# The seven-product form for w_down in a squared-ReLU MLP, and a reordered form for w_up

## The chip, the cores and the metric

The kernel runs on one core of a Trainium2 chip. The metric is the device time of one launch in microseconds: the median of three runs is 1365.35 us for the kernel before (1364.28 to 1368.06). The tensor engine is written TensorE or PE, its weight loads PEld; VectorE is DVE, ScalarE is ACT, GpSimd is POOL; SP is the engine that issues most transfers (DMAs).

## The reference

The program is one step of a two-layer encoder trunk over 640 tokens with a model width of 1024. Each layer has a mixer, a memory attention, projections, and the MLP that the change is about, with a hidden width of 4096:

```
def squared_relu_mlp(x, g_pre, g_post, w_up, w_down):
    a = jnp.square(jax.nn.relu(rmsnorm(x, g_pre) @ w_up))
    return rmsnorm(a @ w_down, g_post)
```

All data are float32, and the kernel keeps that precision: it splits each operand into a high part in the type fp32r, on which TensorE multiplies, and a low part (the operand less its high part), and forms three matmul terms, low by high, high by high and high by low.

## The kernel before

**Tiling.** Tokens are five tiles of 128 (NT), or two halves of 320 (TH). The hidden width is 32 tiles of 128, taken two at a time as 16 pairs (NPAIR). `mlp` runs once for each layer.

**w_up.** The first two pairs of a layer are multiplied in the plain form (`plain`). The other 14 go through the class `Pair`, which uses the Strassen-Winograd form: with two hidden tiles, two halves of the model width and two halves of the tokens, there would be eight products of blocks; the form takes seven, of sums and differences of blocks. A product (`Pair.product`, L597) is 12 matmuls of 320 columns: three terms by four tiles of depth. `Pair.load` makes the sums of the weights s1 to s4 on VectorE (L585 to L588); `head`, `middle`, `second` and `end` run the seven products into six PSUM banks, copy two of the results out on ScalarE (L604, L609) and add the others up in a tile c on VectorE (L612). `end` then makes the squared relu on VectorE and splits it into high and low part.

**w_down.** `down` is plain: for each of the five token tiles, two halves of the model width, the two hidden tiles of a pair and three terms there is a matmul of 512 columns, 60 for a pair (`token_major`, L181, L183, L185); VectorE adds each of the ten sums into y (L701).

**Splits of weights.** `split` (L512, L513) is a cast on ScalarE and a subtraction on VectorE. `summed_parts` does it without VectorE: ScalarE writes the negated cast into the low part, a DMA issued by GpSimd that adds in flight brings the weights on top, and ScalarE casts again:

```
        nc.scalar.mul(lo[:, :w], raw, -1.0)
        nc.gpsimd.dma_start(out=lo[:, :w], in_=src, accum_op=ALU.add)
        nc.scalar.copy(out=hi[:, :w], in_=raw)
```

**Buffers.** Raw weights of 128 x 1024 land in the ring `wraw` of four buffers, by loads on SP's queue. The sums of `Pair.load` take buffers of the same ring. Split weights go into the ring `wring` of eight. PSUM is six short banks (`bank`, named b) and two long ones (`long_bank`, named o).

**What sets the order.** The loop runs `pair.whole()`, the w_down of the pair before, and the load of the next pair. A scheduler turns the program into one fixed queue for each engine when it is built, with `tc.high_priority` and `tc.issue_after` (in `behind`) as hints; each engine then works its queue strictly in order, and an instruction at its head that waits holds all behind it.

Of the kernel before, what the change touches and what calls it, by code (L numbers as in the profile page):

```python
# [9 lines left out]
F32 = mybir.dt.float32  # L10
# [5 lines left out]
P = 128  # L16
# [21 lines left out]
def trunk_kernel(ctx: ExitStack, tc: tile.TileContext, a: dict, o: dict):  # L38
# [17 lines left out]
    def nm(s):  # L56
        uid[0] += 1
        return f"{s}_{uid[0]}"

    def bank():  # L60
        return ps.tile([P, 512], F32, tag="b", name=nm("b"))

    def long_bank():
        return ps.tile([P, 512], F32, tag="o", bufs=2, name=nm("o"))
# [6 lines left out]
    gfm = const.tile([P, G_END], F32, name="gfm")  # L71
    bfb = const.tile([P, 8], F32, name="bfb")
    mhalf = const.tile([P, 1], F32, name="mhalf")
    memqs = const.tile([P, 4, P], F32, name="memqs")
    nc.vector.memset(mhalf, -0.5)
    warm = const.tile([P, 1], F32, name="warm")
    nc.scalar.activation(out=warm, in_=mhalf, func=AF.Square)
# [134 lines left out]
            marks["dve"] = nc.vector.scalar_tensor_tensor(out=xn, in0=x, scalar=r, in1=gb, op0=ALU.mult, op1=ALU.mult)  # L212
        return xn

    def to_fm(xn, hi, lo, c0):

        for q in range(2):
            acc = bank()
            for k in range(4):
                nc.tensor.transpose(acc[:, k * P:(k + 1) * P], xn[:, (4 * q + k) * P:(4 * q + k + 1) * P], ident)  # L220
            av = acc.rearrange("p (k t) -> p k t", k=4)
            h = hi[:, 4 * q:4 * q + 4, c0:c0 + P]
            nc.scalar.copy(out=h, in_=av)
            nc.vector.tensor_tensor(out=lo[:, 4 * q:4 * q + 4, c0:c0 + P], in0=av, in1=h.bitcast(F32), op=ALU.subtract)  # L224
# [10 lines left out]
        t = 0 if i * P < half[1][0] else 1  # L235
        return t, i * P - half[t][0]

    def tile_to(hs, i, xn, half=HALF, prio=HP):
        t, c0 = where(i, half)
        with tc.high_priority(offset=prio):  # L240
            to_fm(xn, hs[t][0], hs[t][1], c0)

    def gain_tile(cpool, src, tag):
        g = cpool.tile([P, D], F32, tag=tag, bufs=1, name=nm(tag))
# [209 lines left out]
    class OutProj:  # L454
# [32 lines left out]
        def flush(self, parts=None):  # L487

            i, xn = self.late.pop(0)
            with tc.high_priority(offset=HP):  # L490
                views = []
                for q in range(2):
                    acc = bank()
                    for k in range(4):
                        nc.tensor.transpose(acc[:, k * P:(k + 1) * P], xn[:, (4 * q + k) * P:(4 * q + k + 1) * P], ident)  # L495
                    views.append(acc.rearrange("p (k t) -> p k t", k=4))
                if parts:
                    for q in range(2):
                        split(*parts[q], views[q])
                for q in range(2):  # L500
                    dst = self.raw[:, 4 * q:4 * q + 4, i * P:(i + 1) * P]
                    if q == 0:
                        nc.scalar.copy(out=dst, in_=views[q])
                    else:
                        nc.vector.tensor_copy(out=dst, in_=views[q])
# [9 lines left out]
    def mlp(l, proj, x_in, aside, yside, hst, before, finish):  # L515
# [8 lines left out]
        apool = ast.enter_context(pool(f"act{l}", 1, aside))  # L524
        tpool = tst.enter_context(pool(f"blk{l}", 1, aside))

        b1 = (hpool.tile([P, KT, TH], F32R, tag="hi0", name=nm("b1h")), hpool.tile([P, KT, TH], F32R, tag="lo0", name=nm("b1l")))
        b22 = (hpool.tile([P, 4, TH], F32R, tag="hi1", name=nm("b22h")), hpool.tile([P, 4, TH], F32R, tag="lo1", name=nm("b22l")))

        def blk(x, what):  # L530
            return tuple(tpool.tile([P, 4, TH], F32R, tag=f"t{x}{y}", name=nm(f"{what}{y}")) for y in "hl")
# [34 lines left out]
        class Pair:  # L566
# [30 lines left out]
                        nc.tensor.matmul(acc[:, :TH], w[wi][:, k, :], b[bi][:, k, :], start=(f and k == 0), stop=(e and k == 3),  # L597
                                         skip_group_check=not first)

            def head(self):  # L600
                self.t = apool.tile([P, 2, 2, TH], F32, tag="c", bufs=2, name=nm("c"))
                acc = long_bank()
                self.product(self.a11, b11, acc)
                nc.scalar.copy(out=self.t[:, 0, 1, :], in_=acc[:, :TH])  # L604
                self.x = acc

            def second(self):
                self.product(self.a12, b21, self.x, False, True)
                nc.scalar.copy(out=self.t[:, 0, 0, :], in_=self.x[:, :TH])  # L609

            def add(self, out, in0, acc):
                nc.vector.tensor_tensor(out=out, in0=in0, in1=acc[:, :TH], op=ALU.add)  # L612

            def middle(self):
                c12, c21, c22 = self.t[:, 0, 1, :], self.t[:, 1, 0, :], self.t[:, 1, 1, :]
                y, w, self.z = bank(), bank(), long_bank()
                self.product(self.s2, ts[1], y)
                self.add(c12, c12, y)
                self.product(self.s3, ts[2], w)
                self.add(c21, c12, w)  # L620
                self.product(self.s1, ts[0], self.z)
                self.add(c22, c21, self.z)

            def end(self):
                c12, c21 = self.t[:, 0, 1, :], self.t[:, 1, 0, :]
                v = bank()
                self.product(self.a22, ts[3], v)
                self.add(c21, c21, v)
                self.product(self.s4, b22, self.z, False, True)
                self.add(c12, c12, self.z)  # L630
                out = [None, None]
                for x in (1, 0):
                    t = self.t[:, x].rearrange("p h n -> p (h n)")
                    nc.vector.scalar_tensor_tensor(out=t, in0=t, scalar=0.0, in1=t, op0=ALU.max, op1=ALU.mult)
                    out[x] = (apool.tile([P, 640], F32R, tag="ah", bufs=4, name=nm("ah")),
                              apool.tile([P, 640], F32R, tag="al", bufs=4, name=nm("al")))
                    split(*out[x], t)
                return out

            def whole(self):  # L640
                self.head()
                self.middle()
                self.second()
                return self.end()

        ys = []
        gpost = []
# [63 lines left out]
        def plain(pcs, tiles, tmp, h):  # L711

            blocks = (b12, b22) if h else (b11, b21)
            for x, (hi, lo) in enumerate(pcs):
                acc = bank()
                for w, y, first, last in ((hi, 0, True, False), (lo, 0, False, False), (hi, 1, False, True)):
                    for k in range(KT):
                        nc.tensor.matmul(acc[:, :TH], w[:, k * P:(k + 1) * P], blocks[k // 4][y][:, k % 4, :],  # L718
                                         start=(first and k == 0), stop=(last and k == KT - 1))
                r = tmp[x // 2][:, x % 2, h, :]  # L720
                ah, al = (t[:, h * TH:h * TH + TH] for t in tiles[x])
                nc.scalar.activation(out=r, in_=acc[:, :TH], func=AF.Relu)
                nc.scalar.activation(out=ah, in_=r, func=AF.Square)
                nc.vector.tensor_tensor(out=r, in0=r, in1=r, op=ALU.mult)
                nc.vector.tensor_tensor(out=al, in0=r, in1=ah.bitcast(F32), op=ALU.subtract)
                if x == 2 and h == 0:
                    n = 4 * P - TH
                    proj.flush([tuple(y[:, :, n:TH] for y in b) for b in (b12, b22)])


        pcs = [piece(a["w_up"][l, f]) for f in range(4)]
        tiles = [(apool.tile([P, 640], F32R, tag="ah", bufs=4, name=nm("ah")),
                  apool.tile([P, 640], F32R, tag="al", bufs=4, name=nm("al"))) for _ in range(4)]
        tmp = [apool.tile([P, 2, 2, TH], F32, tag="c", bufs=2, name=nm("c")) for _ in range(2)]
        first = dict(marks)
        half_blocks(0, TH)
# [3 lines left out]
        other_blocks()  # L740
        hst.close()
        ypool = yst.enter_context(pool(f"y{l}", 1, yside))
        ready = [tiles[:2], tiles[2:]]
        down((0, 1), ready.pop(0), True, False)
        with behind(*first.values()):
            pair = Pair(2)
            pair.load()
        for c in range(2, NPAIR):
            ready.append(pair.whole())
            if c < NPAIR - 1:  # L750
                down((2 * c - 2, 2 * c - 1), ready.pop(0), False, False)
                pair = Pair(c + 1)
                pair.load()
        tst.close()
        cpool = ast.enter_context(pool(f"chain{3 + l}", 2, aside))
        gpost.append(gain_tile(cpool, a["g_mlp_post"][l], "gp"))
        down(range(2 * NPAIR - 4, 2 * NPAIR), ready[0] + ready[1], False, True)
        yst.close()
        return ast

# [24 lines left out]
    att0 = ExitStack()  # L785
    keep0 = att0.enter_context(pool("keep0", 1))
    memq = keep0.tile([P, 4, 512], F32, name="memq0")
    mk0 = keep0.tile([P, 4, 256], F32, name="mk0")
    mv0 = keep0.tile([P, 2, 512], F32, name="mv0")
    wk = att0.enter_context(pool("wk0", 2))  # L790
# [68 lines left out]
    def windows(g):  # L859
# [10 lines left out]
            nc.gpsimd.tensor_tensor(out=nxt[:, c0:], in0=cur[:, c0:], in1=cur[:, c0 - d:784 - d], op=ALU.add)  # L870
            cur, d = nxt, 2 * d
        sp_, ss_ = u_views(cur)
        head = sm(16, "s16")
        nc.vector.tensor_tensor(out=head, in0=sp_[:, 0:16], in1=cst[:, C_IV + 16 * g:C_IV + 16 * g + 16], op=ALU.mult)
        nc.vector.tensor_tensor(out=head, in0=head, in1=up_[:, 0:16], op=ALU.subtract)
        nc.vector.scalar_tensor_tensor(out=up_, in0=sp_, scalar=1.0 / w, in1=up_, op0=ALU.mult, op1=ALU.subtract)
# [63 lines left out]

    def before0(i):
        if len(late) > 1:
            tile_to(hs1, *late.pop(0), HALF1, 0)

    st1.close()
    st1 = mlp(0, proj, proj.x_out, "left", "right", hst, before0, finish0)
# [26 lines left out]
    fox = ExitStack()  # L973
    fk = fox.enter_context(pool("fk", 1))
    memq = fk.tile([P, 4, 512], F32, name="memq1")
    v = fk.tile([P, 4, 512], F32, name="v1")
    kt = [fk.tile([P, 512], F32, name=f"kt{j}") for j in range(4)]
    q = [fk.tile([P, 512], F32, name="q0")]
# [461 lines left out]
```

## Time and profile before

| | |
|---|---|
| median of three runs | 1365.35 us |
| the profiled execution | 1365.08 us |
| its span | 1363.3 us |
| TensorE busy | 1332.5 us, 98% |
| VectorE busy | 848.0 us, 62% |
| ScalarE busy | 608.8 us, 45% |
| GpSimd busy | 246.5 us, 18% |

The profile is one execution of the program. Busy time counts the operations of an engine and not its waits; the span is the time from the first instruction to the last. The MLP of the second layer runs its pairs in the stretch of 972 to 1230 us, that of the first layer in the same way before it.

### The profile page before, as it was taken

The page shows a single profiled execution, that of the slowest core. Times are in us where ns is not written, and L with a number is a line of the kernel's source. Part 1 is how long each engine was busy: PE and PEld are TensorE (multiplying, and loading weights), DVE is VectorE, ACT ScalarE, POOL GpSimd, SP SyncE. Part 2 cuts the span into 40 slices and gives each one's busy share as a digit, 9 for nine tenths or more (in the row PEclk, how much of TensorE's full clock was granted, in tenths as well). Part 3 has the DMA queues.
Part 4 walks back from the last instruction along what each step waited for, and adds up shares of the span by engine and source line. Part 5 has one row for each costly group of instructions (what it writes and reads, how often), then busy time and mean ns, then how long its engine had stood idle before and what let it go on. Part 6 is the DMA issues. An engine that isn't in the chain of part 4 may idle for free. (4 is left out here: it accounts for less than half of the span.)

```text
span 1363.3 us, 20887 instructions
## 1 busy us (share of the span) xinstructions
PE 1332.5 (98%) x8154; PEld 1175.7 (86%) x8154; DVE 848.0 (62%) x1437; ACT 608.8 (45%) x1015; POOL 246.5 (18%) x252
## 2 busy tenths in 40 slices
PE   7999999999999999998999999999999999999997
PEld 6998878988988998996998786679989988988996
DVE  6657439767557666658634566549766566556646
ACT  6435337544353453444434444447534444443432
POOL 3270002111111111133300212312111111111111
PEclk9999999999999999999999998999999999999999
DMA  7736556575666666575636532736666675675663
GB/s 268 224 84 230 204 199 170 123 170 127 161 160 141 161 143 159 135 201 193 240 128 206 178 117 97 243 126 170 150 152 141 153 167 128 154 167 135 155 155 124
DMA packets 87315, 222.82 MB, mean 163 GB/s; under 512 B 18464, under 2 KB 26144, under 8 KB 87216
## 3 DMA queue, kind: packets, MB, share of 16 engines
q1 hardware_dynamic: 69936, 165.91, 37.0%
q0 software_dynamic: 17280, 55.58, 22.3%
q8 instruction: 64, 1.05, 0.3%
q14 instruction: 35, 0.29, 0.1%
HBM read 203.84 MB, written 17.61 MB: 162 GB/s over the span
## 5 line engine op out<-in xcount | busy, mean ns | idle before, releaser
L155 ACT ACTIVATE wl<-raw 128x1024 fp32r<-128x1024 f32 x120 | 114.9, 959 | 252.5 <-PE b L181 243.5
L181 PE MATMUL b<-wl,ah 128*128 128x512 f32 x632 | 200.1, 397 | 4.8 <-DVE hlo L224 2.0
L701 DVE TENSOR_TENSOR y<-y,b 128x512 f32<-128x512 f32 x278 | 177.9, 680 | 38.6 <-PE b L185 38.2
L183 PE MATMUL b<-wh,ah 128*128 128x512 f32 x632 | 198.0, 394 | 0.0
L185 PE MATMUL b<-wh,al 128*128 128x512 f32 x632 | 198.0, 395 | 0.0
L156 POOL DMA_DIRECT2D wl<-in_w_up x56 | 49.2, 879 | 542.3 <-ACT wl L155 286.8
L181 PEld LDWEIGHTS b<-wl,ah 128*128 128x128 f32 x632 | 117.7, 189 | 32.0 <-ACT ah L512 2.7
L183 PEld LDWEIGHTS b<-wh,ah 128*128 128x128 f32 x632 | 118.9, 188 | 27.7
L185 PEld LDWEIGHTS b<-wh,al 128*128 128x128 f32 x632 | 119.1, 188 | 27.5
L512 ACT CAST wh<-raw 128x1024 fp32r<-128x1024 f32 x56 | 58.8, 1049 | 137.0 <-PE o L597 126.1
L157 ACT CAST wh<-raw 128x1024 fp32r<-128x1024 f32 x120 | 112.8, 940 | 0.0
L612 DVE TENSOR_TENSOR c<-c,b 128x320 f32<-128x320 f32 x84 | 41.0, 488 | 106.3 <-PE b L597 106.3
L148 DVE TENSOR_TENSOR wl<-raw,wh 128x1024 fp32r<-128x1024 f32 (+1 forms) x60 | 77.3, 1299 | 20.0 <-ACT wh L147 19.0
L147 ACT CAST wh<-raw 128x1024 fp32r<-128x1024 f32 (+1 forms) x60 | 62.9, 1049 | 40.8 <-POOL raw L144 11.2
L513 DVE TENSOR_TENSOR wl<-raw,wh 128x1024 fp32r<-128x1024 f32 x56 | 68.6, 1224 | 16.1 <-ACT wh L512 15.4
L144 POOL TENSOR_TENSOR raw<-raw,gfm 128x1024 f32<-128x1024 f32 (+1 forms) x28 | 56.5, 2025 | 101.3 <-issue 47.9
L156 POOL DMA_DIRECT2D wl<-in_w_down x64 | 56.4, 887 | 88.7 <-ACT wl L155 49.0
L200 POOL TENSOR_TENSOR s<-s,mhalf 128x1 f32<-128x1 f32 x40 | 26.2, 654 | 230.9 <-DVE s L448 160.0
L585 DVE TENSOR_TENSOR raw<-raw 128x512 f32<-128x512 f32 x28 | 19.4, 692 | 69.1 <-DMA raw<-in_w_up 69.1
L612 DVE TENSOR_TENSOR c<-c,o 128x320 f32<-128x320 f32 x56 | 27.3, 488 | 46.9 <-PE o L597 46.9
L174 PE MATMUL b<-hhi,wh 128*128 128x384 f32 (+1 forms) x312 | 54.7, 316 | 0.3 <-ACT wh L147 0.3
L181 PE MATMUL b<-wl,cathi 128*128 128x512 f32 x160 | 54.7, 422 | 0.0
(324 smaller groups left out, 2760.7 us busy)
## 6 DMA issues: line engine op xcount, KB each, us to landing
raw<-in_w_up SPq DMA_DIRECT2D x64, 512.0 KB, 4.1
raw<-in_w_down SPq DMA_DIRECT2D x64, 512.0 KB, 5.3
wl<-in_w_down POOLq DMA_DIRECT2D x64, 512.0 KB, 8.3
wl<-in_w_up POOLq DMA_DIRECT2D x28, 512.0 KB, 7.0
raw<-in_w_in SPq DMA_DIRECT2D x16, 512.0 KB, 6.8
raw<-in_w_out SPq DMA_DIRECT2D x16, 512.0 KB, 4.6
t<-in_cmk SPq DMA_DIRECT2D x32, 256.0 KB, 5.6
t<-in_cmv SPq DMA_DIRECT2D x32, 256.0 KB, 4.8
```

Source lines behind the costliest of these rows:

```text
L147: nc.scalar.copy(out=hi[:, :w], in_=raw[:, :w])
L148: nc.vector.tensor_tensor(out=lo[:, :w], in0=raw[:, :w], in1=hi[:, :w].bitcast(F32), op=ALU.subtract)
L155: nc.scalar.mul(lo[:, :w], raw, -1.0)
L156: nc.gpsimd.dma_start(out=lo[:, :w], in_=src, accum_op=ALU.add)
L157: nc.scalar.copy(out=hi[:, :w], in_=raw)
L181: nc.tensor.matmul(accs[q][:, :nh], xh, lo[:, c[q]], start=first, stop=False)
L183: nc.tensor.matmul(accs[q][:, :nh], xh, hi[:, c[q]], start=False, stop=False)
L185: mm = nc.tensor.matmul(accs[q][:, :nh], xl, hi[:, c[q]], start=False, stop=last)
L512: nc.scalar.copy(out=hi, in_=src)
L513: nc.vector.tensor_tensor(out=lo, in0=src, in1=hi.bitcast(F32), op=ALU.subtract)
L612: nc.vector.tensor_tensor(out=out, in0=in0, in1=acc[:, :TH], op=ALU.add)
L701: nc.vector.tensor_tensor(out=yq, in0=yq, in1=accs[q], op=ALU.add)
```

## The change

**w_down in seven products.** For hidden tiles 4 to 27 of each layer, two pairs are now taken together, a turn of the new loop. The four hidden tiles are two blocks by two, the model width two halves of 512, and the first four token tiles two blocks of 256. `Down` makes the sums of the w_down blocks: eight subtractions of 512 columns on VectorE in a turn, into four more buffers of `wraw`, and their splits. `Acts` makes the sums of the activations, on 256 columns. `down_form` runs the seven products for both pairs, 12 matmuls of 512 columns each, and for the fifth token tile 24 plain ones: 108 in a turn, where 120 stood. Each product ends in two adds into y, one for each token tile of a block, and the fifth tile takes two more: 16 adds of 512 columns in a turn where 20 stood.

**w_up's form.** `Pair.products` takes the place of `head` to `end`. The seven products go into three banks; a bank is read (copied by ScalarE, L612, L616, L621) in the middle, and the next product sums on into it. So ScalarE makes three copies of 320 columns and VectorE three adds (L603) instead of two and five, and the squared relu is two operations on ScalarE for each of four blocks (L639, L640, L631, L632).

**Smaller edits.** The first four hidden tiles of w_down run as one block, at the end of which the turns begin; `memqs` and a small tile move to other pools; late transposes go into the long banks, and one is tied behind a named matmul; the tiles of `hpool` are made larger, to hold some of the new operands.

```diff
+            def products(self, acts=None):
+                self.c = apool.tile([P, 2, 2, TH], F32, tag="c", bufs=2, name=nm("c"))
...
+                y, x, z = bank(), bank(), long_bank()
+                self.product(self.a11, b11, y)
+                nc.scalar.copy(out=c11, in_=y[:, :TH])
+                self.product(self.a12, b21, x)
+                self.add(c11, x)
+                self.product(self.s2, ts[1], y, False)
+                nc.scalar.copy(out=c12, in_=y[:, :TH])
+                self.act(c11)
+                if acts:
+                    acts.begin(flat)
+                self.product(self.s1, ts[0], z)
+                nc.scalar.copy(out=c22, in_=z[:, :TH])
+                self.product(self.s3, ts[2], y, False)
+                self.add(c22, y)
+                self.act(c22)
+                self.product(self.s4, b22, z, False)
+                self.add(c12, z)
+                self.act(c12)
...
+                self.product(self.a22, ts[3], y, False)
...
+        class Down:
+            def __init__(self, c):
...
+                for x in range(2):
+                    r = wraw.tile([P, RW], F32, tag="raw", name=nm("raw"))
+                    nc.sync.dma_start(out=r[:, :D], in_=a["w_down"][l, 2 * c + x])
...
+            def sums(self, x):
+                r = wraw.tile([P, RW], F32, tag="raw", name=nm("raw"))
+                p, q = r[:, 0:512], r[:, 512:D]
...
+                if x == 0:
+                    sub(p, self.r12, self.r11)
+                    sub(q, self.r22, p)
...
+            product("a12", "b21", x)
+            adds(0, 0, x)
+            product("s1", "t1", z)
+            adds(2, 1, z)
+            product("s2", "t2p", y, False)
+            adds(0, 1, y)
...
+        for c in range(2, NPAIR, 2):
+            end = c == NPAIR - 2
+            dws = []
+            acts = [plain_acts(two[0].products(), 0) if end else two[0].products(Acts(0))]
+            if not end:
+                dws = [Down(c)]
+                t12, t34 = dws[0].sums(0), dws[0].sums(1)
+                dws[0].plain()
+                dws.append(Down(c + 1))
+                dws[1].plain()
+                dws[0].t1, dws[0].t2p = parts(t12[:, :D])
+            acts.append(plain_acts(two[1].products(), 1) if end else two[1].products(Acts(1)))
+            if not end:
+                t12 = dws[1].sums(0)
...
+                down_form(acts, dws)
```

**The order on the engines.** ScalarE before, from the splits of the summed weights of one pair to those of the next two tiles of w_down. The names are tile<-source with a buffer number; L155 is the negated cast, L157 the second cast, and c<-o copies a bank.

```order
L512 CAST wh_12212<-raw_12206 128x1024 [waits DVE_49,PE_49]
L604 COPY c_11996<-o_11997 128x320 [waits PE_49]
L512 CAST wh_12216<-raw_12207 128x1024 [waits DVE_49,PE_49]
L155 ACTIVATE wl_12221<-raw_12204 128x512 [waits DMAHW1_49,DMASW6_49,PE_49]
L609 COPY c_11996<-o_11997 128x320 [waits PE_49]
L157 CAST wh_12220<-raw_12204 128x512
L155 ACTIVATE wl_12335<-raw_12332 128x1024 [waits DMAHW2_49,DMASW7_49,PE_49]
L157 CAST wh_12334<-raw_12332 128x1024 [waits PE_49,Activation_49]
L155 ACTIVATE wl_12342<-raw_12339 128x1024 [waits DMAHW3_49,DMASW5_49,PE_49]
```

Only two copies from banks stand among these, near their head. In the kernel after, ScalarE in the second half of a turn's first pair, where the third w_down tile (raw_11550) and the fourth (raw_11552) are split, up to the first copy from a bank of the turn's second pair (the c_11571 of L612):

```order
L154 ACTIVATE wl_11555<-raw_11550 128x1024 [waits DMAHW4_49,DMASW2_49,PE_49]
L639 ACTIVATE c_11412<-c_11412 128x320 [waits DVE_49]
L156 CAST wh_11554<-raw_11550 128x1024 [waits PE_49]
...
L632 ACTIVATE c_11412<-c_11412 128x320 [waits Activation_49]
L154 ACTIVATE wl_11560<-raw_11552 128x1024 [waits DMAHW5_49,DMASW1_49]
L511 CAST ah_11409<-c_11412 128x512 [waits Activation_49]
L511 CAST ah_11409<-c_11412 128x256 [waits DVE_49]
L511 CAST ah_11409<-st_11411 128x512 [waits DVE_49]
L156 CAST wh_11559<-raw_11552 128x1024
L511 CAST wh_11564<-raw_11534 128x1024 [waits PE_49]
L612 COPY c_11571<-b_11572 128x320
```

Two negated casts, each of which waits for the load of its tile (DMAHW), now stand ahead of the copy by which TensorE may go on in that bank.

VectorE before, at the loads of a pair (L585 to L588) among the adds into y of the w_down that runs meanwhile:

```order
L585 TENSOR_TENSOR raw_12206<-raw_12204 128x512 [waits DMAHW6_49,DMAHW1_49]
L701 TENSOR_TENSOR y_1_9593<-y_1_9593,b_11888 128x512 [waits PE_49]
L513 TENSOR_TENSOR al_11871<-c_11767,ah_11870 128x640 [waits Activation_49]
L701 TENSOR_TENSOR y_1_9593<-y_1_9593,b_11889 128x512 [waits PE_49]
L586 TENSOR_TENSOR raw_12206<-raw_12206,raw_12197 128x512 [waits DMAHW0_49,DVE_49]
L701 TENSOR_TENSOR y_1_9610<-y_1_9610,b_11904 128x512 [waits PE_49]
```

The same place after, for the second pair of a turn to come (raw_11388 is its second w_up tile), among the adds into y (L722) of the last products of w_down:

```order
L722 TENSOR_TENSOR y_1_9779<-y_1_9779,b_11222 128x512 [waits PE_49]
L722 TENSOR_TENSOR y_1_9750<-y_1_9750,b_11225 128x512 [waits DVE_49,PE_49]
L512 TENSOR_TENSOR wl_11373<-raw_11363,wh_11372 128x1024 [waits Activation_49]
L722 TENSOR_TENSOR y_1_9779<-y_1_9779,b_11226 128x512 [waits DVE_49,PE_49]
L722 TENSOR_TENSOR y_1_9808<-y_1_9808,b_11221 128x512 [waits PE_49]
L587 TENSOR_TENSOR raw_11390<-raw_11388 128x512 [waits DMAHW1_49,Activation_49]
L589 TENSOR_TENSOR raw_11391<-raw_11381,raw_11388 128x512 [waits DMAHW0_49,DVE_49]
L722 TENSOR_TENSOR y_1_9837<-y_1_9837,b_11222 128x512 [waits PE_49]
```

The sums of the weights have moved from among the first adds of a pair's w_down to a place ahead of the last adds of a turn, and the first pair's low part (wl_11373) stands before them.

## Rows read from the trace of the kernel before

**Rows 1.** The page: busy time of each engine, its share of the span, instructions.
```profile
PE 1332.5 (98%) x8154; PEld 1175.7 (86%) x8154; DVE 848.0 (62%) x1437; ACT 608.8 (45%) x1015; POOL 246.5 (18%) x252
```
**Rows 2.** Busy us by stretch: length, PE, PEld, DVE, ACT, POOL, granted clock, DMA share, GB/s.
```profile
972.00:1100.00 128.00, 128.00 (x707) 115.25 (x706) 80.32 (x122) 54.80 (x69) 17.63 (x20) 1.00 0.65 154
```
**Rows 3.** Waits, 972 to 1230: engine, line, releaser: us in total, times, longest.
```profile
ACT wl L155 <- PE b L181: 79.2, 9, 9.0
...
DVE raw L585 <- DMA raw<-in_w_up: 26.7, 10, 3.7
...
PEld b L181 <- DVE y L701: 0.8, 2, 0.4
```
**Rows 4.** The chain of waits: by line, then in order of time (start, us).
```profile
by line: PE o L597 7.0%; PE b L181 6.2%; PE b L183 6.0%; PE b L185 6.0%; PE b L597 5.3%; PE b L718 1.5%; DMA raw<-in_w_up 0.7%; DMA xr<-x 0.6%; issue 0.4%; DVE xr L451 0.4%; PE b L495 0.3%; POOL s L200 0.3%; PE o L1288 0.3%; PE b L1269 0.3%
...
1025.65 1.75 PE o L597 x12
...
1209.12 1.75 PE o L597 x12
```
**Rows 5.** Groups of instructions by form: busy us, mean ns of one | idle before.
```profile
L701 DVE TENSOR_TENSOR y<-y,b 128x512 f32<-128x512 f32 x278 | 177.9, 680 | 38.6 <-PE b L185 38.2
...
L513 DVE TENSOR_TENSOR wl<-raw,wh 128x1024 fp32r<-128x1024 f32 x56 | 68.6, 1224 | 16.1 <-ACT wh L512 15.4
L512 ACT CAST wh<-raw 128x1024 fp32r<-128x1024 f32 x56 | 58.8, 1049 | 137.0 <-PE o L597 126.1 <-PE b L185 8.3 <-DVE raw L586 2.6
...
L513 DVE TENSOR_TENSOR al<-c,ah 128x640 fp32r<-128x640 f32 x56 | 45.7, 818 | 0.8 <-ACT ah L512 0.8
...
L612 DVE TENSOR_TENSOR c<-c,b 128x320 f32<-128x320 f32 x84 | 41.0, 488 | 106.3 <-PE b L597 106.3
...
L325 DVE TENSOR_SCALAR mp<-mp,s 128x256 f32<-128x256 f32 x32 | 9.9, 350 | 0.9
...
L723 ACT ACTIVATE ah<-c 128x320 fp32r<-128x320 f32 x16 | 7.5, 470 | 0.3
```
**Rows 6.** Timeline at 1007 to 1009: start, us, engine, line, operation [idle before].
```profile
1007.37 1.23 DVE L513 TENSOR_TENSOR wl<-raw,wh 128x1024 fp32r<-128x1024 f32 x1 [0.60 <-ACT wh L512]
...
1008.62 0.80 SPq L576 DMA_DIRECT2D raw<-in_w_up  x2
```
**Rows 7.** Raw loads by line, 972 to 1230; last row: two loads at 1191.
```profile
L162 SPq DMA_DIRECT2D raw<-in_w_down x20: 327/328/328, 972.8 to 1211.5; - x20
DMA to landing us min/median/max: 4.7/5.3/6.8
...
L576 SPq DMA_DIRECT2D raw<-in_w_up x20: 327/350/827, 982.5 to 1218.9; - x20
DMA to landing us min/median/max: 3.6/3.7/7.7
...
DMA to landing us min/median/max: 3.8/5.7/7.7
```
**Rows 8.** Timeline of 1009 to 1037: VectorE, ScalarE and TensorE at a pair's start.
```profile
1022.32 0.68 DVE L588 TENSOR_TENSOR raw<-raw,raw 128x512 f32<-128x512 f32 x1
1022.92 3.82 DVE L701 TENSOR_TENSOR y<-y,b 128x512 f32<-128x512 f32 x6
...
1023.38 1.06 ACT L155 ACTIVATE wl<-raw 128x1024 fp32r<-128x1024 f32 x1 [9.02 <-PE b L181]
1024.35 1.03 ACT L157 CAST wh<-raw 128x1024 fp32r<-128x1024 f32 x1
...
1027.25 0.74 PE L597 MATMUL b<-t1h,wh 128*128 128x320 f32 x4
...
1027.45 0.43 ACT L604 COPY c<-o 128x320 f32<-128x320 f32 x1 [0.71 <-PE o L597]
```
**Rows 9.** The page: DMAs that add in flight, issued by GpSimd: KB each, us to landing.
```profile
wl<-in_w_down POOLq DMA_DIRECT2D x64, 512.0 KB, 8.3
wl<-in_w_up POOLq DMA_DIRECT2D x28, 512.0 KB, 7.0
```

## What the change does to the time, predicted before the run

> **What bounds the kernel now.** I read the busy shares first: TensorE is busy 98% of the span, VectorE 62%, ScalarE 45% [rows 1]. Then the stretch in which the MLP of the second layer runs its pairs: in 972 to 1100 us TensorE is busy for all 128.00 us at full granted clock, VectorE for 80.32 and ScalarE for 54.80 [rows 2]. In the waits of 972 to 1230 TensorE has one row, 0.8 us; ScalarE's multiplications of w_down tiles (L155) wait for TensorE alone, for buffers it still reads, and none of them has a row for a transfer; only VectorE waits for one, 26.7 us ahead of L585 [rows 3], and as TensorE goes on meanwhile, that costs nothing. So the pair is bound by TensorE's work. The chain in order of time gives its length: the product of L597 that opens a pair comes back every (1209.12 - 1025.65)/7 = 26.21 us [rows 4]. Seven products of twelve matmuls at 1.76 us [rows 4] are 12.3 us, so the 60 matmuls of 512 columns of w_down take 13.9, or 0.231 us each.
>
> **The change, part by part.** I take two pairs, one turn of the new loop, as the unit: 52.4 us before. There are six turns in a layer, twelve in all.
>
> Removed on TensorE: 108 matmuls of 512 columns stand where 120 stood. A turn of matmuls alone is 14 x 1.76 + 108 x 0.231 = 49.6 us, 2.8 less, and 12 x 2.8 = 33 us in all. That is what the change offers.
>
> Added on VectorE, per turn: 8 sums of w_down blocks and 4 low parts of 512 columns (0.68 each), 4 low parts of 1024 (1.22) and 16 operations on 256 columns; gone are 4 adds into y (0.68), 4 adds of 320 (0.49), and 4 squared relus and 4 low parts of 640 (0.82 each) [rows 5]. An operation on 256 columns in this form is not in the trace: above the 0.35 of a one-input one and below the 0.68 of 512 columns [rows 5]; I take 0.42, near the line through 512 and 1024 columns (0.14 + 0.27). VectorE goes from 52.4 x 80.32/128 = 32.9 to 32.9 + 19.8 - 11.2, about 41 us. ScalarE gets 18 more operations of 320 columns (0.47), 4 casts of 1024 (1.05) and 12 casts of 256 and 512 (0.4 to 0.6, estimated from these two), less 4 of 640 (0.7, likewise): from 22.4 to about 38 [rows 2, 5]. Both stay under 49.6, so by their sums these edits cost nothing: TensorE hides them. But the order on both queues is fixed, and what stands at the head of a queue counts.
>
> Kept in number but moved: the transfers. Per turn there are still 4 raw loads of w_up and 4 of w_down, all in the ring of four raw buffers. Before, w_down took its raw buffers for a multiply and a copy; now its sums take two more per pair, so that a turn draws 16 buffers instead of 12 from the same four. A raw load goes out the moment the last reader of its buffer is done: VectorE's L513 ends at 1008.60, the load starts at 1008.62 [rows 6]. It is of use when it lands, and the landing time X of a half-megabyte load is 4.7 to 6.8 us, middle 5.3, for w_down, and 3.6 to 7.7 for w_up, where the middle of 3.7 is that of loads that come first of two [rows 7]. In the new order of the queues three such loads stand in one circle with the engines' work. I follow it from t = 0, the first product of w_up in a turn (six matmuls of w_down aside), with operations in a row at the spacing that the timeline shows: VectorE 0.60 to 0.64 for 512 columns and about 1.2 for 1024, ScalarE 0.97 for 1024, which is 0.09 less than it lasts, and shorter ones by the same less [rows 8].
> 1. VectorE's last add of w_down ends at 1.1, its low part of 1024 columns after it at 2.3. That frees a buffer, and the second w_down tile of the turn is loaded at 2.3.
> 2. It lands at 2.3 + X. The L704 subtraction that waits for it and the one behind it end 1.3 later and free the buffer of the first tile, into which the third goes: it lands at 3.5 + 2X.
> 3. ScalarE's multiplication of the third tile stands in the queue ahead of the copies from banks of the second pair. Behind it come 13 operations and then the copy of c11: four at 0.97, two of these casts, the rest at 0.3 to 0.55, in sum 8.8. The copy is done at 12.3 + 2X. TensorE's product s2 sums into that bank and so starts then; with no wait it would start after ten products and six matmuls of w_down, at 18.8. With X = 5.3 it starts at 22.9.
> 4. From s2 to the end of the low part of s1 and s2 of the next turn's first pair: 5.5 for the products and the 0.2 after which a bank is read [rows 8], a cast and a low part 2.2, then VectorE in an unbroken row of 17 operations of 512 columns, 7 of 256 and 2 of 1024, 15.6. Sum 23.3, so 35.6 + 2X. This frees a raw buffer for the second w_up tile of the next second pair.
> 5. It lands at 35.6 + 3X. VectorE's subtraction L587 waits for it, and the add that frees the bank of the last half product stands two places behind: 1.9; that half product, 1.4. The next turn begins at 38.9 + 3X.
>
> The reads of a bank between two products that sum into it are otherwise covered: a copy of 0.47 starts 0.2 behind its product [rows 5, 8], and the product between lasts 1.76.
>
> So a turn is the longer of 49.6 and 38.9 + 3X; it breaks even with 52.4 at X = 4.5. The bounds: three loads as fast as the first of two give 50.0, three as slow as the slowest w_down load 59.3. Two of the three are w_down loads with others in flight, for which I take the middle, 5.3; the third is the second of two w_up loads, and I take 5.5, near the middle between 3.7 and 7.7 [rows 7]. Then 38.9 + 16.1 = 55.0, which is 2.6 more than before, and 12 x 2.6 = 31 us. In the last two pairs of each layer, outside the twelve turns, the first tile's multiplication also stands ahead of ScalarE's copy of c12 and holds TensorE some 2 us: 4 us in all.
>
> A quick landing has a page behind it. The Trainium skill (DMA: Bandwidth & Descriptors, Anatomy of one DMA) gives a transfer about 2.0 us plus its bytes at 436 GB/s, fitted for transfers issued by GpSimd; as an estimate by that page half a megabyte lands in 3.2 us, a turn would be TensorE's 49.6, and the kernel would win the whole 33. The trace agrees with it only for a load that comes first of two [rows 7]. The same page (Queues, rings and completion order) says that each DMA engine takes packets from its queues in turn, which fits the slower rows.
>
> The rest: the first four w_down pieces come as one block of five tiles (same matmuls, 10 y adds less in a layer, hidden); the transposes of late tiles move to the two long banks and behind a named matmul; memqs and the s16 tiles move between pools. The transposes that move are on the chain for 0.3% of the span (L495), 4 us [rows 4]: that much could go, or come a second time. I take nothing, as TensorE had work on both sides of them.
>
> **Sum.** 1365.1 (span 1363.3 and 1.8 around it; the median of the runs is 1365.35) + 31 + 4 = 1400 us.
>
> **Rivals.** *The loads land early, and the matmuls are saved.* One mechanism: X below 4.5 in the mean of the three, so that the circle is off the path. For it: in a slower circle loads come apart, not in twos, and a lone one takes 3.7. Against it: per turn 6 accumulating transfers of 512 KB at 7.0 to 8.3 us and 2 of 256 KB are in flight [rows 9], over 50 us of them in a turn, so one nearly always is. At X = 3.7 to 4.0 a turn is 50.0 to 50.9: 12 x 1.5 to 2.4 saved, 1336 to 1347. VectorE as the bound by its sum would be here too: 41 us must stretch by a fifth before it matters.
>
> *Two others are always in flight.* X = 6.8 in all three: 59.3, 12 x 6.9 + 4 = 87 more, 1452. For it: a second load of two took 7.7 [rows 7]. Against: the circle itself spreads them.
>
> *A draw*: X between 4.3 and 4.7, or the circle two microseconds shorter than I add it up. 1361 to 1369.
>
> That the change does not do what it says can be left out: the built program has 144 matmuls of 512 columns fewer.
>
> **How the numbers follow.** The forecast (1370 to 1440) 0.62, its slow rival 0.11, the draw 0.07, the early landing 0.20. A difference under 0.3%, 4 us, can't be told from none. Slower 0.73, same 0.07, faster 0.20. The range leaves out the slow rival and the fast half of the early one: 1345 to 1440; the forecast's own is 1370 to 1440.
>
> **What would show it.** Right: in a turn of about 55 us TensorE waits in the second pair for ScalarE's copy of c11 (L612), and before the last half product of w_down for VectorE's add (L722); ScalarE's multiplication of w_down (L154) waits for a transfer, which it never did; VectorE's L587 and L704 wait for raw loads; TensorE's busy time falls by about 33 us while the span grows. Step 3 is wrong if c11's copy is there before TensorE needs it, step 5 if L587 finds its tile landed. The prediction is wrong if TensorE has next to no waits inside the turns, or if raw loads land in under 4.5 us.

## The result and the profile after

The changed kernel takes 1411.7 us (median of 4 runs, 1407.5 to 1413.5) beside 1365.8 for the kernel before (median of 4): 1.033 times as long, 95% interval 1.0303 to 1.0358. The forecast was 1400, in a range of 1345 to 1440.

Where the 46.1 us between the two profiled spans (1363.3 and 1409.4) lie can be read from the first and last start of the plain matmuls of w_down in each layer, which enclose the pairs. First the kernel before, layer one and two, then the one after (line, matmul, minimum, median and maximum of its length in ns, first to last start):

```profile
L181 PE MATMUL b<-wl,ah x320: 387/392/763, 247.1 to 648.7; 128*128 128x512 f32 x160
...
L181 PE MATMUL b<-wl,ah x312: 387/393/504, 958.9 to 1348.6; 128*128 128x512 f32 x156
```

```profile
L180 PE MATMUL b<-wl,ah x80: 388/396/628, 249.3 to 674.8; 128*128 128x512 f32 x80
...
L180 PE MATMUL b<-wl,ah x72: 388/393/404, 988.5 to 1394.7; 128*128 128x512 f32 x72
```

The stretches grew from 401.6 to 425.5 and from 389.7 to 406.2: 40.4 us together. The other 5.7 lie outside, ahead of the first layer's pairs (2.2) and between the last w_down of the first layer and the first of the second (3.5).

Busy time on the page after, which answers to [rows 1]:

```profile
PE 1325.9 (94%) x8010; PEld 1165.6 (83%) x8010; DVE 912.9 (65%) x1593; ACT 770.9 (55%) x1411; POOL 245.2 (17%) x252
```

There are 144 matmuls fewer, yet TensorE's busy time fell by 6.6 us only. The waits say why it is not busy 98% of the span any more; TensorE over the whole span, then ScalarE and VectorE at 1015 to 1320 (columns as in [rows 3]):

```profile
PE b L599 <- ACT c L612: 43.7, 12, 5.2
...
PE b L730 <- DVE y L722: 2.5, 7, 0.5
```

```profile
ACT wl L154 <- DMA raw<-in_w_down: 24.0, 14, 5.2
```

```profile
DVE raw L704 <- DMA raw<-in_w_down: 10.6, 8, 2.0
...
DVE raw L587 <- DMA raw<-in_w_up: 1.5, 3, 0.6
```

TensorE waits twelve times, once in a turn, 3.6 us in the mean, for ScalarE's copy of c11. ScalarE's multiplications of w_down, which waited for TensorE alone in [rows 3], now wait for their loads. The queue of ScalarE shows the two together (start, us, operation, idle before it):

```profile
1082.75 1.06 ACT L154 ACTIVATE wl<-raw 128x1024 fp32r<-128x1024 f32 x1 [2.83 <-DMA raw<-in_w_down]
...
1087.87 1.06 ACT L154 ACTIVATE wl<-raw 128x1024 fp32r<-128x1024 f32 x1 [1.09 <-DMA raw<-in_w_down]
1088.84 0.91 ACT L511 CAST ah<-c 128x512 fp32r<-128x512 f32 x2
1089.65 0.61 ACT L511 CAST ah<-st 128x512 fp32r<-128x512 f32 x1
1090.17 1.04 ACT L156 CAST wh<-raw 128x1024 fp32r<-128x1024 f32 x1
1091.12 1.04 ACT L511 CAST wh<-raw 128x1024 fp32r<-128x1024 f32 x1
1092.06 0.42 ACT L612 COPY c<-b 128x320 f32<-128x320 f32 x1
```

The first row is the third tile of w_down, the second the fourth; the copy for which TensorE waits comes 4.2 us behind the fourth, after five casts.

The chain of waits, with the product that waits for the copy at the two ends of five turns and raw loads of the first four between, answers to [rows 4]:

```profile
1037.73 2.03 PE b L599 x12
...
1059.91 1.15 DVE wl L512
1061.07 4.22 DMA raw<-in_w_up
...
1069.15 4.23 DMA raw<-in_w_down
...
1079.07 8.72 DMA raw<-in_w_down
...
1134.37 8.46 DMA raw<-in_w_down
...
1181.82 4.62 DMA raw<-in_w_down
...
1187.89 7.43 DMA raw<-in_w_down
...
1229.31 4.65 DMA raw<-in_w_up
...
1245.27 6.16 DMA raw<-in_w_down
...
1315.41 3.57 PE b L599 x12
```

A turn of the second layer lasts (1315.41 - 1037.73)/5 = 55.5 us. In the first layer the same product stands five turns apart at

```profile
299.89 0.96 PE L599 MATMUL b<-t1h,wh 128*128 128x320 f32 x4 [3.07 <-ACT c L612]
...
581.14 1.43 PE L599 MATMUL b<-t1h,wh 128*128 128x320 f32 x4 [4.47 <-ACT c L612]
```

which makes a turn of 56.25. In the first of the five turns three raw loads stand in series in the chain, 17.2 us together as it counts them, and in the fifth again three (16.4); in the turns between, which begin at 1092.5, 1147.6 and 1204.0, it holds one (8.5), two (12.1) and two (10.8). The loads themselves, at 1015 to 1320, w_down then w_up, beside [rows 7]:

```profile
DMA to landing us min/median/max: 3.1/5.6/8.8
```

```profile
DMA to landing us min/median/max: 3.1/3.2/3.3
```

A second cost is in the clock. TensorE around the wait that ends at 1092.5, first its matmuls, then stretches of 2 us (columns as in [rows 2]):

```profile
1092.53 1.44 PE L599 MATMUL b<-t1h,wh 128*128 128x320 f32 x4 [3.94 <-ACT c L612]
...
1095.86 0.75 PE L599 MATMUL o<-b22hi,wh 128*128 128x320 f32 x4
```

```profile
1090.00:1092.00 2.00, 0.00 (x0) 0.00 (x0) 1.10 (x3) 2.00 (x3) 0.22 (x1) 1.00 0.59 86
1092.00:1094.00 2.00, 1.47 (x5) 1.47 (x6) 1.81 (x3) 0.95 (x4) 0.00 (x0) 0.60 0.92 176
1094.00:1096.00 2.00, 2.00 (x9) 2.00 (x9) 1.11 (x2) 0.79 (x2) 0.00 (x0) 0.55 0.00 0
1096.00:1098.00 2.00, 2.00 (x16) 2.00 (x15) 0.65 (x2) 1.68 (x3) 0.00 (x0) 1.00 0.00 0
```

After 3.94 us without work the granted clock is 0.55 to 0.60, near the lower of its two levels (1.2 of 2.4 GHz), for about 3 us: the product that opens there takes 3.3 us where twelve matmuls take 1.76. That is 1.6 us more of busy time in a turn.

### The profile page after: what moved, and what is told of

Its sections match the earlier page's. It is cut to its first block, busy times and chain, and to the rows that moved or that the text cites. A ratio compares the mean times of both kernels' runs of the same rounds, so it can differ in the third digit from the quotient of the medians.

```text
span 1409.4 us, 21204 instructions
## 1 busy us (share of the span) xinstructions
PE 1325.9 (94%) x8010; PEld 1165.6 (83%) x8010; DVE 912.9 (65%) x1593; ACT 770.9 (55%) x1411; POOL 245.2 (17%) x252
## 3 DMA queue, kind: packets, MB, share of 16 engines
q0 software_dynamic: 17280, 55.58, 22.9%
## 5 line engine op out<-in xcount | busy, mean ns | idle before, releaser
L511 ACT CAST wh<-raw 128x1024 fp32r<-128x1024 f32 x104 | 109.1, 1050 | 141.1 <-PE b L730 68.6
L512 DVE TENSOR_TENSOR wl<-raw,wh 128x1024 fp32r<-128x1024 f32 x104 | 126.1, 1222 | 32.4 <-ACT wh L511 32.4
L155 POOL DMA_DIRECT2D wl<-in_w_up x56 | 49.1, 877 | 492.3 <-PE b L730 232.5
L722 DVE TENSOR_TENSOR y<-y,b 128x512 f32<-128x512 f32 x168 | 114.9, 684 | 9.3 <-PE b L730 6.7
L730 PE MATMUL b<-wl,ah 128*128 128x512 f32 x288 | 114.3, 397 | 2.6 <-DVE y L722 2.5
L730 PE MATMUL b<-wh,al 128*128 128x512 f32 x288 | 113.6, 394 | 0.0
L730 PE MATMUL b<-wh,ah 128*128 128x512 f32 x288 | 113.5, 394 | 0.0
L156 ACT CAST wh<-raw 128x1024 fp32r<-128x1024 f32 x120 | 113.0, 942 | 0.0
L155 POOL DMA_DIRECT2D wl<-in_w_down x64 | 56.5, 885 | 189.3 <-ACT c L639 89.4
L599 PE MATMUL b<-t1h,wh 128*128 128x320 f32 x112 | 26.9, 370 | 43.7 <-ACT c L612 43.7
L730 PEld LDWEIGHTS b<-wl,ah 128*128 128x128 f32 x288 | 54.0, 188 | 16.8 <-DVE y L722 6.2
L730 PEld LDWEIGHTS b<-wh,al 128*128 128x128 f32 x288 | 54.1, 188 | 12.0
L730 PEld LDWEIGHTS b<-wh,ah 128*128 128x128 f32 x288 | 54.1, 188 | 11.2
L704 DVE TENSOR_TENSOR raw<-raw,raw 128x512 f32<-128x512 f32 x72 | 47.7, 689 | 19.9 <-DMA raw<-in_w_down 19.1
```

The source lines that it names most:

```text
L511: nc.scalar.copy(out=hi, in_=src)
L512: nc.vector.tensor_tensor(out=lo, in0=src, in1=hi.bitcast(F32), op=ALU.subtract)
L704: sub = lambda out, in0, in1: nc.vector.tensor_tensor(out=out, in0=in0, in1=in1, op=ALU.subtract)
L722: nc.vector.tensor_tensor(out=yq, in0=yq, in1=acc, op=ALU.add)
L730: nc.tensor.matmul(accs[r], t[ti][:, s], w[wi], start=(first and x == 0 and f), stop=(e and x == len(ms) - 1), skip_group_check=not first)
```

## The experiments

| run | what is different | median us | ratio to before, 95% interval |
|---|---|---|---|
| changed kernel | | 1411.7 | 1.033 [1.0303, 1.0358] |
| e1 | copy of c11 ahead on ScalarE's queue | 1369.9 | 1.0036 [1.0004, 1.0068] |
| e2 | sums of w_down written over the raw tiles | 1350.6 | 0.9897 [0.9872, 0.9923] |
| e3 | the wait filled with matmuls | 1416.5 | 1.0375 [1.0342, 1.0409] |
| e4 | the new w_up form with plain w_down | 1371.0 | 1.0049 [1.0032, 1.0065] |
| e5 | no adding DMAs of w_down in the turns | 1353.5 | 0.9902 [0.9878, 0.9925] |
| e6 | e2, and the sums of w_up in place | 1340.1 | 0.9815 [0.9787, 0.9843] |
| e7 | e2, late transposes put back | 1360.9 | 0.9961 [0.9946, 0.9976] |
| e8 | e2 with the copy of e1 | 1346.9 | 0.9854 [0.983, 0.9877] |
| e9 | e6 with the copy of e1 | 1331.4 | 0.9749 [0.9723, 0.9774] |

Each ratio is to runs of the kernel before beside it (medians 1363.8 to 1367.2). All start from the changed kernel.

**e1, the place of the copy.**

```diff
-                nc.scalar.copy(out=c11, in_=y[:, :TH])
+                with tc.high_priority(offset=100):
+                    nc.scalar.copy(out=c11, in_=y[:, :TH])
```

> The copy of c11 (L612) stands on ScalarE's queue ahead of the negated cast of the fourth w_down tile, but still behind that of the third; nothing else is changed. Theory Q (the head of ScalarE's queue: the cast that waits for the fourth tile's load holds the copy, TensorE waits 43.7 us in all and works at half clock for some 1.6 us after each of twelve waits): the wait at the copy falls from 43.7 us to under 8 and the time to 1350 to 1365. Theory P (as predicted, the third tile's load sets it): the copy is held as before, over 25 us of waits stay and the time is 1395 to 1415. Theory B (VectorE and ScalarE simply have too much to do): 1405 to 1418.

1369.9 us. Of the three theories Q comes nearest, but its numbers were missed: 13.1 us of waits stay at c11 where it had under 8, and the time is above its range. (The 1.6 us in it is what the slow product costs; the low clock itself lasts about 3 us.) The copy now stands ahead of the fourth tile's multiplication and behind the third's; two casts of activations that stood behind the fourth's have moved ahead of it too. TensorE's waits are (the first at c11, the second at c12):

```profile
PE b L599 <- ACT c L613: 13.1, 11, 2.3
PE b L599 <- ACT c L617: 8.9, 11, 1.3
```

So 30 of the 43.7 us at c11 go with the place behind the fourth tile's split, and 13 stay behind the third's, which the prediction named. But 8.9 come up at c12, whose copy stands behind the fourth's split, so that 22.0 remain in all.

**e2, fewer draws on the raw ring.**

```diff
-                r = wraw.tile([P, RW], F32, tag="raw", name=nm("raw"))
...
-                    sub(p, self.r12, self.r11)
-                    sub(q, self.r22, p)
...
+                sub(self.r11, self.r12, self.r11)
+                sub(self.r12, self.r22, self.r12)
+                sub(self.r22, self.r22, self.r11)
+                sub(self.r21, self.r21, self.r22)
```

> The four sums of a w_down pair are written over the raw tiles themselves, after their splits, so that a turn draws 12 buffers from the raw ring and not 16. The order of copies and casts on ScalarE stays. Theory Q/P (loads late because the ring is drawn too often): raw loads of w_down go out earlier, ScalarE's waits for them fall to under half, the wait at the copy of c11 from 43.7 us to under 15, time 1350 to 1385. Theory B: the same operations, no change, 1405 to 1418, or longer as the sums now wait for casts.

1350.6 us; theory B fell: VectorE and ScalarE are about as busy as in the changed kernel (911.6 and 764.1 us beside 912.9 and 770.9), and the time is 61 us less. The edit also changes which sums are split together, with the same number of operations. A w_down load takes no less than before the edit, 5.7 us at the median of the whole execution beside 5.5. The rows are the waits of TensorE at 1000 to 1300 for the copies of c12 and c11, and two pieces of the chain five turns apart:

```profile
PE b L599 <- ACT c L616: 1.1, 2, 0.8
...
PE b L599 <- ACT c L612: 0.2, 1, 0.2
```

```profile
1020.74 16.70 PE b L730 x72
...
1272.01 6.93 PE b L730 x30
```

A turn is 50.25 us. The multiplications of w_down still stand ahead of the copies; with loads that go out in time that costs nothing.

**e3, is the half clock on the path?**

```diff
+                for _ in range(fill):
+                    nc.tensor.matmul(z, self.a11[0][:, :P], self.a12[0], start=True, stop=True)
                 self.product(self.s2, ts[1], y, False)
```

> 14 more matmuls of 512 columns, of no use, stand on TensorE's queue in each turn just ahead of the product that waits for the copy of c11: 14 x 0.231 = 3.2 us, inside the wait of 3.6. Theory K (the wait costs twice, in itself and by the half clock after it): the product s2 runs at full clock again, 12 x 1.6 = 19 us less, 1388 to 1398, though TensorE does 39 us more of work. If the clock after the wait is not on the path: 1408 to 1416. If TensorE's work sets the turn: 1440 to 1452.

1416.5 us; theory K fell. The clock did come back: in ten of the twelve turns the product runs at full speed.

```profile
PE 1349.9 (95%) x8178; PEld 1182.0 (84%) x8178; DVE 910.5 (64%) x1593; ACT 778.9 (55%) x1411; POOL 246.5 (17%) x252
```

168 matmuls were added, 38.8 us at 0.231, and TensorE's busy time grew by 24.0, so 14.8 us of slow matmuls were saved. But the time stayed, as the intervals overlap: TensorE still waits for the copy (18.0 us), and further on for VectorE's adds into c (9.4, where 2.2 stood). What sets the turn there is seen in the chain, which in each of five turns of the second layer goes through a w_up load and one or two w_down loads; a piece of one:

```profile
1172.90 1.23 DVE wl L512
1174.14 4.26 DMA raw<-in_w_up
...
1179.79 0.61 DVE raw L588
1180.39 0.61 DVE y L724
...
1181.04 3.06 PE b L732 x12
```

This is steps 4 and 5 of the prediction: a low part frees a raw buffer, the w_up tile lands, the subtractions run, the add frees the bank of the last half product.

**e4, the w_up form alone.** The two pairs of a turn go one at a time again, with the plain w_down of before; `products` stays.

```diff
-                down_form(acts, dws)
...
+                    down((2 * c - 2, 2 * c - 1), acts[0], False, False)
```

> The new w_up form (banks read on the way) with the plain w_down for every pair, one pair at a time as before the change. Theory Q/P: no sums of w_down, so the ring is drawn 12 times in two pairs as before and no load holds the copies: 1360 to 1372, no TensorE wait over 1 us at L612. Theory U (reading a bank between products costs in itself, 0.5 to 1.5 us at each of three reads of a pair): 28 pairs x 1.5 to 3 us, 1405 to 1450.

1371.0 us, and no TensorE wait for a copy of a bank in it has a row; theory U fell. The 7 us over the kernel before lie outside the pairs:

```profile
L180 PE MATMUL b<-wl,ah x320: 387/394/480, 249.2 to 651.2; 128*128 128x512 f32 x160
...
L180 PE MATMUL b<-wl,ah x312: 387/393/404, 966.7 to 1355.3; 128*128 128x512 f32 x156
```

402.0 and 388.6 us there, beside 401.6 and 389.7. What costs lies ahead of the pairs (249.2 where 247.1 stood) and between the layers (315.5 where 310.2 stood), where only the smaller edits differ. But e6 has the same smaller edits, and by the same rows its pairs begin at 247.6 us and 309.2 lie between its layers: the edits need not cost anything by themselves. Between the layers the profiles of the kernels that share them spread from 309.2 to 318.5 us.

**e5, the landing time.**

```diff
-                    blocks(*summed_parts(self.raw[x][:, :D], a["w_down"][l, 2 * self.c + x])) for x in range(2))
+                def two_parts(raw):
...
+                    nc.scalar.mul(lo[:, :D], raw, -1.0)
+                    nc.scalar.copy(out=hi[:, :D], in_=raw)
```

> Left out: the four adding DMAs of w_down in each turn (its low parts stay the negated casts). ScalarE's queue, the sums and the draws on the raw ring are those of the changed kernel. Theory X (the landing time of the raw loads carries the stall; the fourth tile's load takes 8.7 us because it shares the DMA engines with these transfers): the w_down loads fall from a median of 5.6 us to about 4, the waits at the copy of c11 from 43.7 us to under 12, the time to 1345 to 1375. Theory R (the ring alone: buffers come free too late, whatever a load takes): over 25 us of these waits stay, 1390 to 1412.

1353.5 us; theory X held. Landing of w_down at 1015 to 1300, and TensorE's wait at c11 over the span:

```profile
DMA to landing us min/median/max: 3.2/3.9/5.5
```

```profile
PE b L599 <- ACT c L612: 6.5, 8, 1.2
```

With the same ring and the same queues of ScalarE, loads of 3.9 us at the median make a turn with little wait. That is the prediction's early rival, which it had put at X below 4.5. The run takes away whatever waited for the adding transfers themselves, too; but among the waits of the changed kernel at 1015 to 1320 no engine has a row for them. Its low parts lack the weights, so only its time is of use.

**e6, all sums in place.**

```diff
...
+                nc.vector.tensor_tensor(out=a22, in0=a21, in1=a22, op=ALU.add)
+                nc.vector.tensor_tensor(out=a21, in0=a11, in1=a21, op=ALU.subtract)
+                nc.vector.tensor_tensor(out=a11, in0=a22, in1=a11, op=ALU.subtract)
+                nc.vector.tensor_tensor(out=a12, in0=a12, in1=a11, op=ALU.subtract)
```

> As e2, and the four sums of a w_up pair are written over their raw tiles too: a turn draws 8 buffers from the raw ring. Theory Q: e2 has next to no stall left, so little more is to be had: 1340 to 1352. Theory B2 (the sums now wait for the casts of w_up on ScalarE, and the first product of a turn that needs them comes late): 1355 to 1380.

1340.1 us, as Q expected. In a stretch of the turns TensorE has no gap, and the chain is TensorE alone:

```profile
1050.00:1100.00 50.00, 50.00 (x279) 44.79 (x278) 40.64 (x66) 34.17 (x58) 7.08 (x8) 1.00 0.70 158
```

```profile
1009.36 15.32 PE b L728 x66
...
1209.17 15.30 PE b L728 x66
```

A turn is 199.81/4 = 49.95 us.

**e7, the late transposes back.**

```diff
-                    if x == 3 and h == 0 and y == 0 and w is hi:
...
+                if x == 2 and h == 0:
...
-            tile_to(hs1, *late.pop(0), HALF1, CP, long_bank)
+            tile_to(hs1, *late.pop(0), HALF1, 0)
```

> As e2, with the late transposes as in the kernel before the change (short banks, behind the third tile of the plain form, no tie to a named matmul, priority 0 for those between the layers). Theory T (the smaller edits cost the 7 us by which e4 is slower than before, as waits of TensorE at the moved transposes and in the plain form): 1342 to 1347. If they cost nothing: 1349 to 1353.

1360.9 us: 0.65% slower than e2 by the ratios, against theory T, and above both ranges. TensorE waits at the transposes for VectorE, where e2 has 5.0 us of such waits in all:

```profile
PE b L494 <- DVE xn L211: 12.1, 4, 5.6
```

The pairs begin at 253.8 us, where those of e2 begin at 247.5: this is the larger part of the 9.9 us between the two profiled spans. The new place saves time where the rest of the change stands. What costs the 7 us of e4 is open.

**e8 and e9, both edits together.** The diffs are those of e1 on e2 and on e6.

> As e2, and the copy of c11 goes ahead of the splits on ScalarE's queue, as in e1. With the sums in place TensorE waits 2.6 us in all for copies, so theory Q expects no gain: 1347 to 1354. If the order of the copies still mattered by itself (8.9 us of waits at the copy of c12 in e1): 1352 to 1362.

> As e6, with the copy of c11 ahead of the splits on ScalarE's queue as in e1 and e8. In e6 the turns take 49.98 us with TensorE busy all the time, so theory Q leaves nothing to gain: 1336 to 1343. If the copy's place is worth by itself the 3.7 us by which e8 is below e2: 1333 to 1338.

1346.9 us, no loss, at the lower end of what Q expected; and 1331.4 us, below both ranges. The intervals of e6 and e9 do not overlap, though the profiled span of e9 (1334.7) is only 1.4 below that of e6 (1336.1). The first and last start of the plain matmuls of w_down tell more: from the one to the other the layers take 387.3 and 371.4 us in e9, 391.7 and 372.9 in e6, so 5.9 less, while 5.1 more lie between the layers in the execution that was profiled, which is the slowest of e9's four (1336.5; the others 1330.7 to 1331.5). So the copy's place is worth something beside the sums in place: a turn of the second layer is 49.67 us where e6 has 49.95, and at the end of the first layer's pairs TensorE waits 3.4 us for splits of activations where e6 has 6.8. Why these waits are shorter was not found. e9 is the fastest version: 2.5% under the kernel before.

## Why the prediction came out so

**The mechanism: right in kind. Its sum: near, in part by luck.** A turn was put at 55.0 and is 55.5 in the second layer and 56.25 in the first. That raw loads come late, hold ScalarE's ordered queue and so the copy that TensorE needs, is shown: e2 (fewer draws on the ring) and e5 (shorter landings) each take most of the loss away and leave the other cause as it was, e1 takes most of it by the order of the queue alone, and a turn without stalls is 49.95 in e6, where matmuls alone were put at 49.6. The circle of the second and third w_down tile and a w_up tile, 38.9 + 3X with 3X = 16.1, is not found whole in any of the five turns. The chain holds 17.2, 8.5, 12.1, 10.8 and 16.4 us of raw loads in them, 13.0 in the mean, and not those three together; where it holds less, TensorE's own work stands in it, as from 1092.5 to 1131.7 without a break. The landing time was the deciding unknown; it was taken from the loads of before [rows 7], and of the three loads the third tile's came near it (5.6 to 7.4), while the second's (4.1 to 4.7) and the w_up ones (3.1 to 3.3) were quicker. That the turn still came within 1.3 us of the sum is luck in part.

**Step 3: right in place, half right in the tile.** The copy that TensorE waits for was put at 22.9 us after the turn's first product. In the turn that starts at 1125.4 it is 22.2:

```profile
1125.38 5.13 PE b L599 x35
...
1147.57 3.30 PE b L599 x12
```

But in three of the five turns, this one among them, the last load in the chain is the fourth tile's, whose multiplication stands five casts ahead of the copy. Only in the other two, whose waits end at 1204.0 and 1260.2, is it the third's, 13 operations ahead, as predicted. The fourth tile's load was not followed at all; in the five turns it lands after 8.3 to 8.8 us, beyond the slowest load of [rows 7], 7.7, beside the third tile's and the adding transfers. e1 divides the two: 30 us at c11 go with the fourth, 13 stay with the third.

**Steps 4 and 5: on the path in three of five turns, and mis-sized.** The w_up load was taken at 5.5 and takes 3.2, and L587 hardly waits (1.5 us in all), which by the prediction's own sign puts step 5 close to wrong; the w_down loads were taken at 5.3 and reach 8.8. So the wait lies at the copy (43.7) and not before the last half product (2.5). The Trainium skill (DMA: Bandwidth & Descriptors, Anatomy of one DMA) has a fit for transfers issued by GpSimd, by which such a load is estimated at 3.2 us. The w_up loads of the kernel after, issued by SP, agree with it (3.1 to 3.3); the w_down loads, with others in flight, take up to 2.7 times as long.

**TensorE's busy time: wrong.** It was to fall by 33 us and fell by 6.6. The step that failed is the one that priced a wait at its own length: each is followed by slow matmuls, 1.6 us a turn, which makes 19 of the 26 us that did not come. In e6, with next to no waits in the turns, the busy time is 1301.8 us, 30.7 below the kernel before, so the matmuls themselves were priced right. The Trainium skill (TensorE: Matmul & The Clock Gate, HAM oscillation) describes such kernels, in which waits for transfers bring the clock down again and again; the rows at 1092 to 1096 us above, 0.55 to 0.60 granted after 3.94 us without work, agree. It did not spoil the time, as e3 shows: with most of the clock back the kernel is no faster, as loads set the turn there.

**The rest of the sum: 11 us short.** 35 were forecast and 46 came. The pairs took 40.4, of which the ten turns timed above make 5 x 3.1 + 5 x 3.85 = 34.8 over the 52.4 of before, where 10 x 2.6 = 26 were forecast; the first turns and the last pairs make the other 5.6, where 9 were. And 5.7 came outside the pairs, where the prediction took nothing and left 4 either way. e4, which has the smaller edits and no stall in the pairs, has 7.4 there; e6, with the same edits, has none. The range of the draw, 1361 to 1369, does not follow from its X: 4.3 to 4.7 gives 7 us either way and the 4 of the last pairs, 1362 to 1376. Nothing else was built on it.

**VectorE and ScalarE** were put at 41 and 38 us a turn; e6 shows 40.6 and 34.2 in 50 us. Neither was the bound there.

## What to carry to other kernels

Before work is moved from a full engine to others, count the draws on each ring of buffers and write down which load stands in front of which instruction of an ordered queue: late loads ahead of one copy here cost more than 144 matmuls saved. Where sums of loaded data take buffers of the same ring, writing them over the data after its last use gives the loads back their lead: the same arithmetic went from 3.3% slower than before to 1.9% faster (e6). And a load's time is to be taken from rows in which as many transfers are in flight as there will be.

## What was not expected of the hardware

A raw load of half a megabyte landed in 3.1 us at the least and 8.8 at the most in the same stretch of one kernel; without the adding transfers of w_down the most was 5.5. After a wait of 3.94 us TensorE's granted clock was 0.55 to 0.60 for some 3 us. Useless matmuls in part of such waits kept the product behind them at full speed in ten of twelve turns without making the kernel faster (1416.5 beside 1411.7 us).
